# Second out-projection tile prepared among the last input-projection units, and the two blocks of the second half swapped

## The chip, the cores and the metric

The kernel runs on one core of a Trainium2 chip. The metric is the time of one execution in device microseconds (us); lower is better. TensorE (PE) does the matrix products, VectorE (DVE) and ScalarE (ACT) the elementwise work, GpSimd (POOL) small powers and masks, SyncE (SP) issues the DMA transfers.

## The reference

One layer of a hybrid backbone runs over 256 context tokens and 2048 latent tokens of width 1024. Each token is normalised and modulated, and one input projection makes z, the SSD input xbc, dt, and the three conformer inputs ga, gb and gsil. The SSD group scans in both directions; the conformer group convolves. Both meet in one output projection:

```
h = rms_norm(x, g_pre) * (1 + scale) + shift
z, xbc, dt_raw, ga, gb, gsil = split(h @ w_in)
y_ssd  = rms_norm((scan_fwd + scan_bwd + d_skip * xs) * silu(z), norm_g)
y_conf = silu(layer_norm(depthwise_conv(ga * sigmoid(gb)))) * silu(gsil)
out = x + gate * rms_norm(concat(y_ssd, y_conf) @ w_out, g_post)
```

The backward scan runs from the last token to the first. The final scan states of the context are outputs as well.

## The kernel before

All matrix products are made of three float32r products each (high x high, low x high, high x low), so every weight exists as a high part (wh, woh) and a low part (wl, wol).

**Tokens.** 18 tiles of 128 tokens lie in five blocks (`TOK`, `BNS`): block 0 is the context, blocks 1 to 4 are 512 latent tokens each. The input projection runs in two halves, blocks 1, 2, 0 and then 3, 4 (`ORDER`). The normalised input of a block (hh and hl) lies in one of three buffer pools, `hps[SLOT[b]]`. When a pool is closed (`ph_b[...]`), its space goes to what is opened next, once its last reader is done.

**Input projection.** A unit makes 128 output channels for every block of the half, 24 matmuls of 128x512 a block (`mm_cm`). `silu_unit` is such a unit for z and gsil: Tanh on ScalarE, a product on VectorE (tile sth), and a store to a DRAM buffer (zs or gs). The helper yields after each k, so the matmuls of a block are followed by its Tanh and store only when the unit is taken up again. The last three gs units of the second half (`last`, j = 5, 6, 7) run block by block: all three for the first block, then all three for the second.

**Out-projection.** Tiles go backwards through the latent tokens, 17, 16, ... 2, then 1, 0 (`order`); tiles 17 and 16 both lie in block 4. For each tile the kernel

- loads y, z, the decays el, ct and the stored state st (`ssd_load`, `st_load`),
- adds the carried backward state Sb: `state_mm` (16 matmuls, banks qo), `y_state`, then `y_gate` and `y_sum` (product with z, squares, their sum over channels, tile zr), `state_decay` and `state_add`,
- loads the conformer output cn and normalises it: `conf_load`, `conf_sum`, `conf_mean` (bank cm), `conf_centre`, `conf_square`, `conf_sqsum` (tile nq),
- gets the two scale factors in `norms` (matmuls to pm, a power on POOL) and `spread` (matmuls to pn), applies them in `ssd_scale` and `conf_scale`, then `conf_silu` (Silu on ScalarE) and `conf_gate` with the gate gsl that `gs_load` loads back from gs,
- splits the results in high and low parts (yh, yl and ph, pl), and multiplies with 16 weights, 8 with yh, yl and 8 with ph, pl (`out_part`).

Weights are loaded by `load_wo`: a load to a staging buffer wst, a cast to woh on ScalarE and a subtraction to wol on VectorE. wst shares its two tags, of two buffers each, with yh and yl; even weights use the one, odd weights the other. Weights 0 to 8 come during the input projection; 9 to 15 go into pool wo4, which takes the space of the input projection's pools after the last unit. Buffers nq and gsl exist once, cn, v, y and z twice.

**Order.** Up to the loop over `order` the kernel is scheduled when it is built: a planner with an estimate of each instruction's duration orders the instructions of each engine and queue, the earlier in the program first among those that it holds ready. The order is then fixed, and each engine and queue works through its own. In the loop VectorE, ScalarE and TensorE keep program order (`V.on = S.on = T.on = True`); those instructions carry line 77 in the profile. At the start of a tile the loop does the first weight, then `norms` of the next tile.

Of the kernel before, what the change touches and what calls it, by code (L numbers as in the profile page):

```python
# [27 lines left out]
TOK = (0, 256, 768, 1280, 1792)  # L28
BNS = (256, 512, 512, 512, 512)
ORDER = ((1, 2, 0), (3, 4))  # L30
SLOT = (0, 1, 2, 1, 2)
RAWO = (2, 260, 772, 130, 642)
NF = 3
PREP = 16
Z0, XBC0, DT0, GA0, GB0, GS0 = 0, 1024, 2560, 2592, 3616, 4640
# [26 lines left out]
def take(gen, n):  # L62
    for _ in range(n):
        yield next(gen, None)
# [16 lines left out]
def backbone_kernel(ctx, tc, xa, xt_in, cols, rows, wconv, conf_b, gp_row, bg_row, state0, w_mod, w_dt, w_in, w_out,  # L81
# [19 lines left out]
    GS = [dram(f"gs{h}", [D, HT[h] * P]) for h in range(2)]  # L101
# [458 lines left out]
    def silu_unit(half, c0, dst, j, hb, order=None):  # L560
        w = next_w()
        for b in order or ORDER[half]:
            BN, o = BNS[b], TOK[b] - half * HT[0] * P
            ps = bank("mm", f"sp{half}_{c0}_{j}_{b}")
            yield from mm_cm(ps, w, hb[b])
            th = ev(f"sth{half}_{c0}_{j}_{b}")[:, :BN]
            S.activation(th, ps[:, :BN], AF.Tanh, scale=0.5)  # L567
            V.scalar_tensor_tensor(th, th, 1.0, ps[:, :BN], ADD, MUL)  # L568
            DMA.dma_start(dst[half][j * P:(j + 1) * P, o:o + BN], th)
# [308 lines left out]
    def run(gen):  # L878
        for _ in gen:
            pass  # L880
# [5 lines left out]
    hb = {}  # L886
# [30 lines left out]
    xbc_phase(0, first, hb, [hprep(2, hb), hprep(0, hb)], tails, dt_post(0))  # L917
    extra = chain([gate_rows()] + [ctx_conv(j, big) for j in range(4)])
    interleave(post(0, 6), merge(scan(range(9)), 68, extra, 9 + 4 * 13), 90 * 8)
    last = [silu_unit(0, GS0, GS, j, hb, (1, 2, 0)) for j in (6, 7)]  # L920
    prep = hprep(3, hb)
    s = 0
    for b in range(3):
# [67 lines left out]
    def ssd_load(i):  # L991

        first = i == NCTX - 1
        t = sl[i] = {}
        if not first:
            t["ct"] = p1.tile([P, 2, P], F32, tag="ct", name=f"ct{i}", bufs=1)
            DMA.dma_start(t["ct"], xb_slice(i, 10, 2))
            t["el"] = p1.tile([P, 8, P], F32, tag="el", name=f"elb{i}", bufs=1)
            decay_rows(t["el"], i, 1)
        t["y"] = p1.tile([P, 8, P], F32, tag="y", name=f"y{i}", bufs=2)  # L1000
        DMA.dma_start(t["y"].rearrange("p q l -> p (q l)"), YP[i])
        t["z"] = p1.tile([P, 8, P], F32, tag="z", name=f"z{i}", bufs=2)
        DMA.dma_start(t["z"], chan_slice(ZS, i))

    def st_load(i):
        sl[i]["st"] = p1.tile([P, D], F32, tag="st", name=f"stl{i}", bufs=1)
        DMA.dma_start(sl[i]["st"], ST[i])

    def state_mm(i):
        if i != NCTX - 1:  # L1010
            sl[i]["po"] = [bank("ss", f"qo{i}{g}") for g in range(2)]
            for g, po in enumerate(sl[i]["po"]):
                for q in range(4):
                    T.matmul(po[:, q * P:(q + 1) * P], Sb[g][:, q * P:(q + 1) * P], sl[i]["ct"][:, g, :],
                             start=True, stop=True)

    def state_decay(i, g):
        if i != NCTX - 1:
            for h in range(8):
                cs = slice(h * HD, (h + 1) * HD)  # L1020
                S.activation(Sb[g][:, cs], Sb[g][:, cs], AF.Copy, scale=eTb[:, i, 8 * g + h:8 * g + h + 1])

    def state_add(i):
        for g in range(2):
            sg = sl[i]["st"][:, g * 512:(g + 1) * 512]
            if i == NCTX - 1:
                V.tensor_copy(Sb[g], sg)
            else:
                V.tensor_tensor(Sb[g], Sb[g], sg, ADD)

    def y_state(i):
        if i != NCTX - 1:
            el, y = sl[i]["el"], sl[i]["y"]
            for g, po in enumerate(sl[i]["po"]):
                gs = slice(4 * g, 4 * g + 4)
                V.tensor_tensor(el[:, gs, :], el[:, gs, :], y8(po), MUL)
            V.tensor_tensor(y, y, el, ADD)

    def y_gate(i):
        y, z = sl[i]["y"], sl[i]["z"]  # L1040
        V.tensor_tensor(y, y, z, MUL)
        S.activation(z, y, AF.Square)

    def y_sum(i):
        z = sl[i]["z"]
        zr = p1.tile([P, P], F32, tag="zr", name=f"zr{i}", bufs=1)
        return sl[i]["y"], sum8(zr, z[:, 0:4, :], z)
# [6 lines left out]
    def norms(i, yz, nq):  # L1054

        pm = bank("ss", f"pm{i}")
        src = [(c, e, t[1]) for c, e, t in ((0, 4.0 * EPS, yz), (1, EPS, nq)) if t]
        for c, e, t in src:
            T.matmul(pm[:, c:c + 1], t, ones[:, 0:1], start=True, stop=True)
        rs = []  # L1060
        for c, e, t in src:
            ms = p1.tile([P, 1], F32, tag=f"ms{c}", name=f"yms{i}{c}", bufs=2)
            V.tensor_scalar(ms, pm[:, c:c + 1], 1.0 / D, e, MUL, ADD)
            rs.append((c, rstd_of(p1, ms, f"yr{i}{c}")))
        return rs

    def spread(i, rs):
        pb = bank("ss", f"pn{i}")
        for c, r in rs:
            T.matmul(pb[:, c * P:(c + 1) * P], r.to_broadcast([P, P]), ident, start=True, stop=True)  # L1070
        return pb
# [7 lines left out]
    def lo(t):  # L1079
        V.tensor_tensor(t[1], t[2], t[0].bitcast(F32), SUB)  # L1080
# [6 lines left out]
    order = list(range(NT - 1, NCTX - 1, -1)) + [1, 0]  # L1087
# [8 lines left out]
    def conf_load(i):  # L1096
        n = p2.tile([P, 8, P], F32, tag="cn", name=f"cn{i}", bufs=2)
        DMA.dma_start(n, CV[:, i * P:(i + 1) * P].rearrange("(c p) t -> p c t", p=P))
        return n

    def conf_sum(i, n):
        v = p2.tile([P, 8, P], F32, tag="v", name=f"v{i}", bufs=2)
        return v, sum8(v[:, 0, :], v[:, 0:4, :], n)

    def conf_mean(i, t):
        mean = bank("ss", f"cm{i}")[:, 0:P]
        T.matmul(mean, ones, t, start=True, stop=True)
        return mean

    def conf_centre(n, mean):  # L1110
        V.scalar_tensor_tensor(n, rows8(mean), -1.0 / D, n, MUL, ADD)

    def conf_square(v, n):
        S.activation(v, n, AF.Square)
        return v

    def conf_sqsum(i, v):
        return v, sum8(p2.tile([P, P], F32, tag="nq", name=f"nq{i}", bufs=1), v[:, 0:4, :], v)

    def gs_load(i):  # L1120
        gs = p2.tile([P, 8, P], F32, tag="gs", name=f"gsl{i}", bufs=1)
        DMA.dma_start(gs, chan_slice(GS, i))
        return gs

    def conf_scale(n, pb):
        V.tensor_tensor(n, n, rows8(pb[:, P:2 * P]), MUL)

    def conf_silu(n, v):
        for k in range(8):
            S.activation(v[:, k, :], n[:, k, :], AF.Silu, bias=cv[:, C_LNB + k:C_LNB + k + 1],  # L1130
                         scale=cv[:, C_LNG + k:C_LNG + k + 1])

    def conf_gate(v, gs):
        V.scalar_tensor_tensor(v, v, 0.5, gs, MUL, MUL)
# [46 lines left out]
    i = order[0]  # L1181
# [7 lines left out]
    yz = y_sum(i)  # L1189
    for g in range(2):  # L1190
        state_decay(i, g)
    state_add(i)
    run(take(blocks, 5))
    for k in range(6, 9):
        load_wo(k, wo2)
        run(take(blocks, 8))
    run(blocks)
    last = [silu_unit(1, GS0, GS, j, hb) for j in range(5, 8)]
    for b in range(2):
        for m, u in enumerate(last):  # L1200
            run(take(u, 8))
            if b == 0 and m == 1:
                rs = norms(i, yz, None)
            if b == 1 and m == 0:
                ssd_scale(i, yz[0], spread(i, rs))
                yh = hl(p0, "y", 2, i, yz[0])
                lo(yh)
                ph_b[1].close()
                p2 = ph_1.enter_context(tc.tile_pool(name="p2", bufs=1))
                n = conf_load(i)  # L1210
                v, t = conf_sum(i, n)
                conf_centre(n, conf_mean(i, t))
    for u in last:
        run(u)
    v, nq = conf_sqsum(i, conf_square(v, n))
    conf_scale(n, spread(i, norms(i, None, (v, nq))))
    gs = gs_load(i)
    conf_silu(n, v)
    conf_gate(v, gs)
    ph_b[2].close()  # L1220
    ph_h.close()
    p3 = ph_1.enter_context(tc.tile_pool(name="p3", bufs=1))
# [1 line left out]
    for k in range(9, 16):  # L1224
        load_wo(k, wo4)
    load_gg(0)
    i = order[1]
    ssd_load(i)
    st_load(i)
    n = conf_load(i)  # L1230
    state_mm(i)
    y_state(i)
    y_gate(i)
    yz = y_sum(i)
    for g in range(2):
        state_decay(i, g)
    v2, t = conf_sum(i, n)
    conf_centre(n, conf_mean(i, t))
    nq = conf_sqsum(i, conf_square(v2, n))
    gs = gs_load(i)  # L1240
    ssd_load(order[2])
    n2 = conf_load(order[2])
    V.on = S.on = T.on = True
    for a, i in enumerate(order):
        last = a + 1 == NT
# [5 lines left out]
        rs = None if last else norms(nxt, yz, nq)  # L1251
# [7 lines left out]
        if nx2 is not None:  # L1259
            st_load(nx2)  # L1260
            v2, t = conf_sum(nx2, n2)
# [5 lines left out]
        if nxt is not None:  # L1267
# [4 lines left out]
            v = nq[0]  # L1272
# [18 lines left out]
        if nx2 is not None:  # L1291
            y_gate(nx2)
            state_decay(nx2, 1)
            gs = gs_load(nx2)
            nq = conf_sqsum(nx2, v2)
        if a:
            finish_add(order[a - 1])
        if nx2 is not None:
            yz = y_sum(nx2)
        if a + 3 < NT:  # L1300
            ssd_load(order[a + 3])
            n, n2 = n2, conf_load(order[a + 3])
        else:
            n = n2
# [72 lines left out]
```

## Time and profile before

| | |
|---|---|
| median of 3 runs | 1872.1 us (1870.85 to 1872.3) |
| profiled execution | 1872.28 us, span from first to last instruction 1870.5 us |
| TensorE granted clock, mean | 0.984 |
| PE busy | 1808.1 us, 97% of the span |
| DVE, ACT, POOL busy | 1203.1, 863.8, 175.9 us |
| DMA | 375.22 MB, mean 201 GB/s |
| input projection's last unit matmul | at 1404.67 us |
| first out-projection matmul | at 1408.31 us |

Rows of a timeline are: start, duration, engine, line, operation, tile written <- tiles read, and in brackets the idle time of the engine just before, with what ended it. SPq and ACTq are the queues of SyncE and ScalarE. A row with a count (x2) merges neighbours of the same kind. Rows of a chain are: start, duration, what the end of the program was waiting for then. Rows of a stretch are: stretch, its length, then the busy time of each engine with its number of instructions, the granted TensorE clock, the DMA engines' busy share and GB/s.

### The profile page before, as it was taken

Reading aid. Unit: us, or ns where it says so; the run is one execution under the profiler, and the core shown is the slowest. Engines: PE = TensorE matmul, PEld = TensorE weight load, DVE = VectorE, ACT = ScalarE, POOL = GpSimd, SP = SyncE. Lnnn points to the kernel's source line nnn. Section 1 sums busy time; section 2 is a strip of 40 time slices with the busy share of each in tenths; the row PEclk is TensorE's granted clock in tenths of the full one; section 3 lists DMA queues with packets and bytes.
Section 4 is the critical chain, followed back from the end, with each engine's and each line's share of the span. In section 5 each row is a group of like instructions: output and inputs, shape, how many; then the busy total and the mean of one; then the engine's idle time right before and its main releaser. Section 6 shows DMA issues by size and latency. Waiting matters only on the chain.

```text
span 1870.5 us, 30012 instructions
## 1 busy us (share of the span) xinstructions
PE 1808.1 (97%) x11223; PEld 1493.1 (80%) x11223; DVE 1203.1 (64%) x1841; ACT 863.8 (46%) x1956; POOL 175.9 (9%) x281
## 2 busy tenths in 40 slices
PE   7899999999999999999998989999997999999998
PEld 4788887788888888888876767777886888888887
DVE  2477887785555553577587845666347777777773
ACT  3646424455445441644224545553326454444441
POOL 0002001111101100100001111110000111111110
PEclk9899999999999999999999999999998999999999
DMA  8656575576566654545589798895967656666632
GB/s 298 219 199 210 203 241 181 175 254 219 195 217 211 226 196 169 167 155 189 170 200 233 199 251 229 258 244 175 331 189 209 183 167 174 172 171 178 182 106 79
DMA packets 305309, 375.22 MB, mean 201 GB/s; under 512 B 85254, under 2 KB 204678, under 8 KB 305164
## 3 DMA queue, kind: packets, MB, share of 16 engines
q1 hardware_dynamic: 284428, 335.56, 58.1%
q10 hardware_dynamic: 20736, 37.76, 7.1%
q8 instruction: 88, 1.44, 0.3%
q14 instruction: 57, 0.47, 0.1%
HBM read 243.66 MB, written 129.59 MB: 200 GB/s over the span
## 4 chain that ended last, share of the span: by engine, by line
PE 85%; DMA 7%; DVE 4%; ACT 1%; issue 1%; SPq 1%; POOL 0%; POOLq 0%; DVEq 0%; ACTq 0%
PE op L77 21%; PE sp L391 7%; PE sp L392 7%; PE sp L393 7%; PE xp L391 5%; PE xp L392 5%; PE xp L393 5%; PE ga L391 3%; PE ga L393 2%; PE ga L392 2%; PE gb L391 2%; PE gb L393 2%; PE gb L392 2%; DMA lb<-lt 2%; PE py L732 2%; DVE cg L608 2%
## 5 line engine op out<-in xcount | busy, mean ns | idle before, releaser
L696 ACT ACTIVATE lb<-lb,WB 128x128 f32<-128x128 f32 x576 | 184.3, 391 | 167.7 <-POOL lb L688 162.1
L391 PE MATMUL sp<-hh,wh 128*128 128x512 f32 (+1 forms) x640 | 238.5, 373 | 0.0
L392 PE MATMUL sp<-hl,wh 128*128 128x512 f32 (+1 forms) x640 | 236.0, 369 | 0.0
L393 PE MATMUL sp<-hh,wl 128*128 128x512 f32 (+1 forms) x640 | 235.8, 368 | 0.0
L391 PE MATMUL xp<-hh,wh 128*128 128x512 f32 (+1 forms) x480 | 179.3, 375 | 6.1 <-ACT wh L366 4.9
L688 POOL TENSOR_SCALAR_AFFINE_SELECT lb<-lb 128x512 f32<-128x512 f32 x144 | 112.6, 786 | 714.2 <-ACT el L685 366.7
L393 PE MATMUL xp<-hh,wl 128*128 128x512 f32 (+1 forms) x480 | 179.0, 373 | 0.0
L392 PE MATMUL xp<-hl,wh 128*128 128x512 f32 (+1 forms) x480 | 178.9, 373 | 0.0
L488 DVE SCALAR_TENSOR_TENSOR cva<-raw,cwh,cva 128x1280 f32<-128x1280 f32 (+1 forms) x96 | 142.1, 1488 | 19.7 <-ACT cva L482 17.9
L391 PEld LDWEIGHTS sp<-hh,wh 128*128 128x128 f32 x640 | 120.6, 189 | 20.8 <-DVE sth L568 0.4
L393 PEld LDWEIGHTS sp<-hh,wl 128*128 128x128 f32 x640 | 120.6, 188 | 20.7
L392 PEld LDWEIGHTS sp<-hl,wh 128*128 128x128 f32 x640 | 120.7, 189 | 19.8
L391 PE MATMUL ga<-hh,wh 128*128 128x512 f32 (+1 forms) x320 | 122.0, 381 | 6.8 <-DMA wh<-whd 6.3
L391 PE MATMUL gb<-hh,wh 128*128 128x512 f32 (+1 forms) x320 | 121.4, 379 | 5.3 <-DVE gth L555 5.3
L393 PE MATMUL ga<-hh,wl 128*128 128x512 f32 (+1 forms) x320 | 119.4, 373 | 0.5 <-DMA wl<-wld 0.5
L392 PE MATMUL gb<-hl,wh 128*128 128x512 f32 (+1 forms) x320 | 119.6, 374 | 0.0
L393 PE MATMUL gb<-hh,wl 128*128 128x512 f32 (+1 forms) x320 | 119.6, 374 | 0.0
L392 PE MATMUL ga<-hl,wh 128*128 128x512 f32 (+1 forms) x320 | 119.2, 373 | 0.0
L568 DVE SCALAR_TENSOR_TENSOR sth<-sth,sp 128x512 f32<-128x512 f32 (+1 forms) x80 | 50.4, 630 | 97.3 <-ACT sth L567 96.9
L391 PEld LDWEIGHTS xp<-hh,wh 128*128 128x128 f32 x480 | 92.1, 192 | 23.2 <-ACT wh L366 5.5
L608 DVE SCALAR_TENSOR_TENSOR cg<-cg,cv 128x256 f32<-128x256 f32 x240 | 107.6, 487 | 0.6
L392 PEld LDWEIGHTS xp<-hl,wh 128*128 128x128 f32 x480 | 91.7, 191 | 15.7 <-DVE hl L312 0.4
(252 smaller groups left out, 3745.8 us busy)
## 6 DMA issues: line engine op xcount, KB each, us to landing
lb<-lt ACTq DMA_DIRECT2D x144, 256.0 KB, 4.5
wr<-in_w_in SPq DMA_DIRECT2D x88, 256.0 KB, 4.7
whd<-wh SPq DMA_DIRECT2D x44, 512.0 KB, 3.6
wld<-wl SPq DMA_DIRECT2D x44, 512.0 KB, 5.2
wh<-whd SPq DMA_DIRECT2D x44, 512.0 KB, 4.6
wl<-wld SPq DMA_DIRECT2D x44, 512.0 KB, 5.8
xT<-xb SPq DMA_DIRECT2D x18, 512.0 KB, 5.0
yp<-yg SPq DMA_DIRECT2D x36, 256.0 KB, 4.3
```

Of the source, the lines that this page charges most:

```text
L77: return lambda *a, **k: self._tc.keep_in_program_order(f(*a, **k))
L391: T.matmul(ps[:, :BN], wh[:, k, :], hh[:, k, :], start=(k == 0), stop=False)
L392: T.matmul(ps[:, :BN], wh[:, k, :], hl[:, k, :], start=False, stop=False)
L393: T.matmul(ps[:, :BN], wl[:, k, :], hh[:, k, :], start=False, stop=(k == KT - 1))
L488: V.scalar_tensor_tensor(a[:, :n], raw[:, t:t + n], cwh[:, ct * 5 + t:ct * 5 + t + 1], a[:, :n], MUL, ADD)
L568: V.scalar_tensor_tensor(th, th, 1.0, ps[:, :BN], ADD, MUL)
L608: V.scalar_tensor_tensor(acc, g[:, t:t + 256], cv[:, w0 + t:w0 + t + 1], acc, MUL, ADD)
L688: G.affine_select(E[g, hq, d], E[g, hq, d], pattern=[[0, 4], [sg, P]], compare_op=ALU.is_ge, fill=NEG, base=0, channel_multiplier=-sg)
L696: S.activation(lb[:, h, :], lb[:, h, :], AF.Exp, bias=WB[:, i, c + h:c + h + 1])
L732: T.matmul(py[g][j * HD:(j + 1) * HD, q * P:(q + 1) * P], xt[g][:, h * HD:(h + 1) * HD], E[g, hq, 0][:, t, :], start=True, stop=True)
```

## The change

Tile 17 is `order[0]` (i), tile 16 is `order[1]` (i1).

- `SLOT` gives block 3 the pool that block 4 had, and the other way round. The last units of the second half do block 4 before block 3, and those of the first half block 2 before block 1, so that the pool that comes free first is the one that is taken first, as before.
- `ssd_load` and `st_load` of tile 16 stand right after tile 17's `state_add`, no longer behind the weight loads.
- `state_mm`, `y_state` and `y_gate` of tile 16 stand after the second unit of the first block, its `y_sum` and `state_decay` after the third, where tile 17's `ssd_scale` and the split into yh, yl now stand too (they stood one unit later).
- Pool p2 is opened after the third unit of the first block. Both tiles' `conf_load`, `conf_sum`, `conf_mean`, `conf_centre` and `conf_square` stand there, and tile 17's `conf_sqsum`.
- Among the second block's units come tile 17's `norms` with tile 16's `conf_sqsum`, then tile 17's `spread`, `conf_scale` and `conf_silu`, then tile 17's `gs_load` and `conf_gate` and tile 16's `gs_load`. Tile 17's part of this stood behind the last unit, tile 16's behind the weight loads.

Nothing is added to or left out of the computation, and the loop is the same.

```diff
-SLOT = (0, 1, 2, 1, 2)
+SLOT = (0, 1, 2, 2, 1)
...
-    last = [silu_unit(0, GS0, GS, j, hb, (1, 2, 0)) for j in (6, 7)]
+    last = [silu_unit(0, GS0, GS, j, hb, (2, 1, 0)) for j in (6, 7)]
...
     state_add(i)
+    i1 = order[1]
+    ssd_load(i1)
+    st_load(i1)
     run(take(blocks, 5))
...
-    last = [silu_unit(1, GS0, GS, j, hb) for j in range(5, 8)]
+    last = [silu_unit(1, GS0, GS, j, hb, (4, 3)) for j in range(5, 8)]
     for b in range(2):
         for m, u in enumerate(last):
             run(take(u, 8))
             if b == 0 and m == 1:
                 rs = norms(i, yz, None)
-            if b == 1 and m == 0:
+                state_mm(i1)
+                y_state(i1)
+                y_gate(i1)
+            if b == 0 and m == 2:
                 ssd_scale(i, yz[0], spread(i, rs))
                 yh = hl(p0, "y", 2, i, yz[0])
                 lo(yh)
+                yz = y_sum(i1)
+                for g in range(2):
+                    state_decay(i1, g)
                 ph_b[1].close()
                 p2 = ph_1.enter_context(tc.tile_pool(name="p2", bufs=1))
-                n = conf_load(i)
-                v, t = conf_sum(i, n)
-                conf_centre(n, conf_mean(i, t))
+                nn = [conf_load(i), conf_load(i1)]
+                vv = [conf_sum(j, n) for j, n in zip((i, i1), nn)]
+                for (v, t), j, n in zip(vv, (i, i1), nn):
+                    conf_centre(n, conf_mean(j, t))
+                    conf_square(v, n)
+                nq = conf_sqsum(i, vv[0][0])
+            if b == 1 and m == 0:
+                rs = norms(i, None, nq)
+                nq = conf_sqsum(i1, vv[1][0])
+            if b == 1 and m == 1:
+                n, v = nn[0], vv[0][0]
+                conf_scale(n, spread(i, rs))
+                conf_silu(n, v)
+            if b == 1 and m == 2:
+                gs = gs_load(i)
+                conf_gate(v, gs)
+                n = nn[1]
+                gs = gs_load(i1)
     for u in last:
         run(u)
-    v, nq = conf_sqsum(i, conf_square(v, n))
-    conf_scale(n, spread(i, norms(i, None, (v, nq))))
-    gs = gs_load(i)
-    conf_silu(n, v)
-    conf_gate(v, gs)
     ph_b[2].close()
     ph_h.close()
...
     load_gg(0)
-    i = order[1]
-    ssd_load(i)
-    st_load(i)
-    n = conf_load(i)
-    state_mm(i)
-    y_state(i)
-    y_gate(i)
-    yz = y_sum(i)
-    for g in range(2):
-        state_decay(i, g)
-    v2, t = conf_sum(i, n)
-    conf_centre(n, conf_mean(i, t))
-    nq = conf_sqsum(i, conf_square(v2, n))
-    gs = gs_load(i)
     ssd_load(order[2])
```

## The prediction, made before the changed kernel ran

> **What bounds the kernel now.** I read the page first, then the chain of work that ended last, then stretches around the place that the diff touches, then each engine's timeline there. TensorE (PE) is busy nearly throughout, so only time in which PE stands still, or runs slowly, can be won. The page's first row, and the chain where it leaves PE:
>
> ```profile
> PE 1808.1 (97%) x11223; PEld 1493.1 (80%) x11223; DVE 1203.1 (64%) x1841; ACT 863.8 (46%) x1956; POOL 175.9 (9%) x281
> ...
> 1406.44 5.36 DMA gs<-sth
> 1411.85 4.33 DMA gsl<-gs
> 1417.42 2.36 DVE wol L976 x2
> 1422.20 0.98 PE pm L77 x4
> ```
>
> Between the last input-projection unit and the first out-projection tile the chain runs over two transfers in a row: the store of the last gate block, then the load of it back. The stretches (us, PE, PEld, DVE, ACT, POOL, granted clock, DMA share):
>
> ```profile
> 1389.00:1409.94 20.94, 20.06 (x101) 16.63 (x99) 13.59 (x21) 6.91 (x16) 0.55 (x1) 1.00 0.69 208
> 1409.94:1422.20 12.26, 0.00 (x1) 0.03 (x1) 8.38 (x12) 10.00 (x20) 0.00 (x0) 0.60 0.97 234
> 1422.20:1426.40 4.20, 4.20 (x13) 3.52 (x14) 1.60 (x4) 2.10 (x2) 0.22 (x1) 0.54 0.94 312
> ...
> 1447.50:1472.40 24.90, 24.90 (x124) 20.95 (x123) 19.10 (x30) 13.19 (x36) 2.67 (x3) 1.00 0.75 196
> ```
>
> PE does nothing for 12.26 us, and the 4.2 us behind it run at a clock of 0.54. The last row is one whole out-projection tile later: no gap. PE's own timeline gives the marks:
>
> ```profile
> 1404.67 0.39 PE L393 MATMUL sp<-hh,wl 128*128 128x512 f32 x1
> 1404.90 0.28 PE L1059 MATMUL pm<-ones,nq 128*128 128x1 f32 x2
> 1406.06 0.49 PE L1070 MATMUL pn<-ident,yr 128*128 128x128 f32 x2 [0.88 <-POOL yr L148]
> 1406.38 1.95 PE L1014 MATMUL qo<-ct,Sb 128*128 128x128 f32 x16
> 1408.17 0.39 PE L1107 MATMUL cm<-v,ones 128*128 128x128 f32 x2
> 1408.31 0.70 PE L77 MATMUL op<-woh,yh 128*128 128x512 f32 x2
> ...
> 1422.20 0.56 PE L77 MATMUL pm<-ones,zr 128*128 128x1 f32 x2 [12.26 <-DVE zr L986]
> ...
> 1447.56 0.61 PE L77 MATMUL op<-woh,yh 128*128 128x512 f32 x2
> ...
> 1461.39 0.70 PE L77 MATMUL op<-woh,ph 128*128 128x512 f32 x2
> ...
> 1471.49 0.62 PE L77 MATMUL op<-wol,ph 128*128 128x512 f32 x2
> 1472.40 0.61 PE L77 MATMUL op<-woh,yh 128*128 128x512 f32 x2
> ```
>
> The first tile (17) takes 1447.56 - 1408.31 = 39.25 us, the next 1472.40 - 1447.56 = 24.84. The excess, 14.41, is the wait of 12.26 and 2.15 of slow clock. PE waits for zr, nq of tile 16, the second tile, because the loop keeps program order and wants them 1.4 us after its start. What delayed them:
>
> ```profile
> 1409.33 1.28 ACT L1130 ACT_TABLE_LOAD   x1
> 1410.62 3.18 ACT L1130 ACTIVATE v<-cn,cv 128x128 f32<-128x128 f32 x8
> ...
> 1416.28 1.23 DVE L1134 SCALAR_TENSOR_TENSOR v<-v,gsl 128x1024 f32<-128x1024 f32 x1 [3.70 <-DMA gsl<-gs]
> ...
> 1421.57 0.28 DVE L986 TENSOR_TENSOR nq<-v 128x128 f32<-128x128 f32 x1
> ```
>
> **The change, part by part.**
>
> *Loads of tile 16.* Their move up costs and wins nothing: SyncE's queue issues them early already, ct, st and both cn here, the cn pair the moment the first block's buffer is free (L1098 is the load, x2 both tiles):
>
> ```profile
> 1358.64 0.39 SPq L997 DMA_DIRECT2D ct<-xb  x1
> ...
> 1362.52 0.57 SPq L1007 DMA_DIRECT2D stl<-st  x1
> ...
> 1388.24 1.00 SPq L1098 DMA_DIRECT2D cn<-cv  x2
> ...
> 1396.70 0.38 PE L1107 MATMUL cm<-v,ones 128*128 128x128 f32 x2
> ```
>
> The fourth row is tile 17's mean, slipped between unit matmuls with no wait beside it: the pattern that the change extends.
>
> *The swapped blocks.* Both tiles lie in block 4, now stored first; its last unit ends three units (3 x 24 matmuls at 0.23 us, some 16 us) before the last matmul, at about 1388 us. So 5.36 + 4.33 us of store and load leave the chain of tile 17's gate. SLOT swaps two equal 512-token buffers; the order in the first half only mirrors this. Zero for both: the same matmuls hide the same loads. Unhidden, either could cost one transfer, about 5 us.
>
> *Tile 16's PE work* (qo 16 matmuls, cm) and tile 17's pm and pn go ahead of the last unit matmuls. PE still does them: from 1404.90 to 1408.31 is 3.41 us, 0.88 of it waiting, so 2.53 us move ahead and the last unit matmul moves from 1404.67 to 1407.20. The loop starts at 1408.31 - 0.88 = 1407.43.
>
> *VectorE, ScalarE and POOL* do the same instructions earlier. Of VectorE's, tile 16's state part (four operations of up to 1.23 us, and a sum) goes where it is nearly idle, and its conformer part into the stretch above where 7.35 us are free:
>
> ```profile
> 1380.00:1390.00 10.00, 10.00 (x47) 8.30 (x46) 1.53 (x3) 1.20 (x2) 0.55 (x1) 1.00 0.12 38
> ...
> 1417.53 0.37 SPq L1122 DMA_DIRECT2D gsl<-gs  x1
> ```
>
> Two waits are added. nq has one buffer, so tile 16's sum of squares waits for tile 17's pm, with VectorE's later work behind it. The gate load gsl has one buffer too, so tile 16's waits on SyncE's queue for tile 17's gate, and the last store or the staging loads may stand behind it; today that load (second row) went out at 1417.53, as the gate ended (1416.28 + 1.23). I take zero for both: up to 5.85 us of lateness inside tile 17 is covered by the weights, next; past it, each us costs one.
>
> Ceiling so far: 14.41 + 0.88 = 15.29 us.
>
> *What is late next: weights 9 to 15 of the out-projection.* Their tiles take the space of the input-projection pools, and ScalarE's sequencer waits for it; then each staging buffer waits for the subtraction two weights earlier:
>
> ```profile
> L975 ACTq EVENT_SEMAPHORE  x3: 17/38/249, 1411.5 to 1411.9; - x3
> ...
> 1415.14 1.97 ACT L975 CAST woh<-wst 128x1024 fp32r<-128x1024 f32 x2
> ...
> 1418.67 1.48 SPq L969 DMA_DIRECT2D wst<-in_w_out  x2
> ...
> 1426.06 0.33 SPq L969 DMA_DIRECT2D wst<-in_w_out  x1
> ...
> 1429.66 2.69 SPq L969 DMA_DIRECT2D wst<-in_w_out  x2
> ...
> 1424.80 1.23 DVE L976 TENSOR_TENSOR wol<-wst,woh 128x1024 fp32r<-128x1024 f32 x1 [2.75 <-ACT woh L975]
> ...
> 1428.42 1.21 DVE L976 TENSOR_TENSOR wol<-wst,woh 128x1024 fp32r<-128x1024 f32 x1
> ...
> 1430.77 1.23 DVE L976 TENSOR_TENSOR wol<-wst,woh 128x1024 fp32r<-128x1024 f32 x1 [0.54 <-ACT woh L975]
> ...
> 1435.38 1.23 DVE L976 TENSOR_TENSOR wol<-wst,woh 128x1024 fp32r<-128x1024 f32 x1 [0.46 <-ACT woh L975]
> 1436.79 1.23 DVE L976 TENSOR_TENSOR wol<-wst,woh 128x1024 fp32r<-128x1024 f32 x1 [0.18 <-ACT woh L975]
> ```
>
> The load at 1426.06, for one, follows the subtraction that ends at 1424.80 + 1.23 = 1426.03. The semaphores came at 1411.5 to 1411.9; the last gate store landed at 1406.44 + 5.36 = 1411.80, so I take it that the casts wait for that store (its source buffer lies in the space). It landed 7.13 us after the last unit matmul, and this link moves with the matmul: 1407.20 + 7.13 = 1414.33 after the change, about when the casts run today. From the first cast to the end of the last subtraction is 1438.02 - 1415.14 = 22.88 us, a relay of four transfers on two buffers; it would end at 1437.21. PE reaches wol of weight 15 at 1471.49 - 1447.56 = 23.93 us after a tile's start, that is at 1431.36. Wait: 5.85 us. Bounds: 0, where the buffers that tile 17's yh and yl hold serve as staging once PE has used them (1461.39 - 1447.56 = 13.83 into the tile, at 1421.26), and 5.85 + 5.74 = 11.6, where the last store is held on ScalarE as well (rival 2). I take 5.85, nearest to the rows: today no staging load uses those buffers either.
>
> Cut by weight (12 is ready 14.49 us after the first cast, 13 after 16.86, 14 after 21.47; PE uses one every 1.38 us, 10.1 us for 7 1/3), the wait falls into about 1.6, 1.0 and 3.2 us. The Trainium skill, "TensorE: Matmul & The Clock Gate", What's actually happening, has the clock halved after an idle window of about 3.4 us and full after as long a busy one. The trace agrees on the first gap, 0.60 and then 0.54 granted. By that rule these pieces would keep the clock; joined, they would cost another 2.15, and the sum would be 1865.
>
> **Sum.** 15.29 - 5.85 = 9.44 us off the profiled execution's own 1872.28, so 1862.84. That execution is 0.18 above the median of the runs, 1872.1; forecast 1862.7.
>
> **The rivals.**
>
> 1. *The weights come in time* (the freed yh/yl buffers serve, or casts start sooner): the whole 15.29, 1857.0. For it: two free buffers are just what the relay lacks. Against: they come free at 1421.26, after four of the seven weights are under way, and the next tile's yh and yl want them too.
>
> 2. *The casts start later still.* Silu of tile 17 now stands ahead of the last units' Tanh in the program. Silu needed a table load (1.28) after a long run of Tanh; interleaved, the last Tanh may wait for 3.18 of Silu and two loads, 5.74 us in all, and the last store, the casts and PE's wait go with it one for one: down to 1868.6. Against: the planner may put Tanh first. The Trainium skill, "ScalarE: Activation LUTs", What ACT_TABLE_LOAD costs, gives a switch about 2.66 us including a drain; by that 8.5 us, and 1871.3. The trace differs: 1409.33 + 1.28 is 1410.61, and Silu starts at 1410.62.
>
> 3. *No change.* The relay ends over 5.8 us later than I have it, say with casts queued behind tile 17's Silu, ph and tile 16's work on ScalarE: first cast near 1420, 1868.6 to 1875. Each us of cast delay is a us of time.
>
> 4. *Slower: PE's queue is held inside the last units.* PE issues in a fixed order. If the planner puts tile 17's mean, pm and pn where it believes them ready, and the data come later, everything behind stops, and last matmul, store and weights all move along. From the cn issue at 1388.24 to pn at 1406.06 is 17.82 us; held for all of it, 1862.84 + 17.82 = 1880.7. It decides from 9.44 us of such waits (13.2 for a loss of 0.2%). For it: pn waited 0.88 even today. Against: cm and tile 17's first pn waited nothing, and 16 us of unit matmuls are there to fill.
>
> **How the numbers follow.** A measurement of this kernel tells about 0.2%, 3.7 us, from no change. Chances: forecast, 1860 to 1865.5, 0.40; rival 1, 1856.5 to 1860, 0.25; rival 2, 1865.5 to 1868.4, 0.17; rival 3, 0.10; rival 4, 0.08. Faster 0.40 + 0.25 + 0.17 = 0.82, same 0.10, slower 0.08. The range that leaves out rivals 3 and 4 is 1856.5 to 1868.5.
>
> **What the profile after would show.** Right: the chain no longer has gsl in it; no PE wait for zr; qo and cm of tile 16 among the unit matmuls; the clock at 1.00 through the change-over; the first tile taking 24.84 us plus a wait for woh or wol of weights 12 to 15; the later tiles still 24.84. Wrong: a wait of PE among the last six unit blocks (rival 4), more than one ACT_TABLE_LOAD near Silu with the last Tanh behind it (rival 2), or no wait for wol at all (rival 1). What would break the forecast whole is a different plan of the queues elsewhere, seen as changed times before 1350.

## The result, and the profile after

The changed kernel is slower: 1883.74 us (1882.67 to 1886.02) against 1872.2 (1870.85 to 1874.19), a ratio of 1.0062 [1.0045, 1.008]. The forecast was 1862.7, faster. The profiled execution took 1884.29, its span is 12.0 us longer than that of before (1882.5 against 1870.5), and all 12 us have come by the end of the first out-projection tile (1459.57 against 1447.56). Busy times on the page are those of before within 4 us; TensorE does the same matmuls:

```profile
PE 1810.8 (96%) x11223; PEld 1495.9 (79%) x11223; DVE 1202.5 (64%) x1841; ACT 864.1 (46%) x1956; POOL 171.9 (9%) x281
```

TensorE's timeline at the change-over:

```profile
1399.94 0.38 PE L1107 MATMUL cm<-v,ones 128*128 128x128 f32 x2
...
1406.09 0.39 PE L393 MATMUL sp<-hh,wl 128*128 128x512 f32 x1
1406.32 0.39 PE L77 MATMUL op<-woh,yh 128*128 128x512 f32 x1
1406.54 0.28 PE L1059 MATMUL pm<-ones,nq 128*128 128x1 f32 x2
1407.70 0.49 PE L1070 MATMUL pn<-ident,yr 128*128 128x128 f32 x2 [0.88 <-POOL yr L148]
1407.94 0.48 PE L77 MATMUL op<-woh,yh 128*128 128x512 f32 x1
...
1409.18 0.28 PE L77 MATMUL pm<-ones,zr 128*128 128x1 f32 x2
...
1413.30 0.61 PE L77 MATMUL op<-woh,yl 128*128 128x512 f32 x2
1438.44 1.40 PE L77 MATMUL pn<-ident,yr 128*128 128x128 f32 x4 [24.52 <-POOL yr L148]
...
1459.57 0.62 PE L77 MATMUL op<-woh,yh 128*128 128x512 f32 x2
```

The old wait is gone: pm of zr, which waited 12.26 us, runs at 1409.18 without one. Four weights into the tile comes a new wait, twice as long: pn of tile 16, the second half of the same two factors. It waits for POOL's power yr, which needs yms, the scaled mean square that VectorE makes from pm. The stretches (us, then PE, PEld, DVE, ACT, POOL, granted clock, DMA share, GB/s) show a TensorE that stands still, a clock that drops for it, and a later tile of the same length as before (24.80 us, without a gap):

```profile
1408.00:1413.90 5.90, 5.90 (x29) 4.61 (x27) 1.22 (x1) 4.36 (x9) 0.00 (x0) 1.00 0.69 210
1413.90:1438.40 24.50, 0.02 (x1) 0.00 (x0) 11.40 (x12) 8.27 (x9) 1.54 (x2) 0.60 0.49 150
1438.40:1443.00 4.60, 4.56 (x15) 3.88 (x16) 4.49 (x8) 1.18 (x2) 0.59 (x1) 0.52 0.31 114
1459.60:1484.40 24.80, 24.80 (x123) 20.90 (x122) 18.66 (x28) 12.36 (x33) 2.68 (x3) 1.00 0.56 159
```

VectorE is busy for less than half of the wait (11.40 of 24.50), and yet yms, 0.2 us of work, does not come through. Its timeline says why:

```profile
1414.04 1.22 DVE L1134 SCALAR_TENSOR_TENSOR v<-v,gsl 128x1024 f32<-128x1024 f32 x1 [4.60 <-ACT v L1130]
1415.84 2.36 DVE L976 TENSOR_TENSOR wol<-wst,woh 128x1024 fp32r<-128x1024 f32 x2 [0.57 <-ACT woh L975]
1423.69 2.50 DVE L976 TENSOR_TENSOR wol<-wst,woh 128x1024 fp32r<-128x1024 f32 x2 [5.49 <-ACT woh L975]
1429.52 1.23 DVE L976 TENSOR_TENSOR wol<-wst,woh 128x1024 fp32r<-128x1024 f32 x1 [3.34 <-ACT woh L975]
1431.87 1.23 DVE L976 TENSOR_TENSOR wol<-wst,woh 128x1024 fp32r<-128x1024 f32 x1 [1.12 <-ACT woh L975]
1435.49 1.22 DVE L976 TENSOR_TENSOR wol<-wst,woh 128x1024 fp32r<-128x1024 f32 x1 [2.39 <-ACT woh L975]
1436.63 0.21 DVE L77 TENSOR_SCALAR yms<-pm 128x1 f32<-128x1 f32 x2
```

Its input pm was there before 1410, and it ran at 1436.63: all seven subtractions of weights 9 to 15 stand ahead of it. Each waits (the brackets) for its cast; the first two casts stand behind tile 17's Silu, the other five wait for transfers. Tile 17's gate (1414.04) stands ahead of yms too, but it ends at 1415.26; from there to 1436.63, 21.4 us, nothing but the subtractions stands ahead of yms. Before, only three subtractions stood ahead. This is the row of before's VectorE timeline; of its subtractions shown in the prediction, the one at 1424.80 is the third, and those at 1428.42, 1430.77, 1435.38 and 1436.79 come behind yms, between the loop's own instructions:

```profile
1425.95 0.21 DVE L77 TENSOR_SCALAR yms<-pm 128x1 f32<-128x1 f32 x2
```

The chain of what ended last, after, is the relay (load, cast and subtraction of one weight after the other) and then yms. It runs through the odd weights 9, 11, 13 and 15: from 11 on, the load of each starts as the subtraction of the one before frees its staging buffer:

```profile
1407.86 3.84 DMA gs<-sth
1411.70 2.32 ACT v L1130 x6
...
1414.76 1.05 ACT woh L975
1415.84 1.24 DVE wol L976
1417.09 5.50 DMA wst<-in_w_out
...
1434.41 1.05 ACT woh L975
1435.49 0.98 DVE wol L976
...
1436.63 0.23 DVE yms L77 x2
1436.86 1.53 POOL yr L148
...
1438.44 1.40 PE pn L77 x4
```

The account against before: 12.26 + 2.15 us go, 24.52 and some 2.2 of slow clock (4.60 x 0.48) come: +12.3, where the spans differ by 12.0.

### The profile page after: what moved, and what is told of

Same layout as the page of the kernel before. It is cut to its first block, busy times and chain, and to the rows that moved or that the text cites. A ratio compares the mean times of both kernels' runs of the same rounds, so it can differ in the third digit from the quotient of the medians.

```text
span 1882.5 us, 30016 instructions
## 1 busy us (share of the span) xinstructions
PE 1810.8 (96%) x11223; PEld 1495.9 (79%) x11223; DVE 1202.5 (64%) x1841; ACT 864.1 (46%) x1956; POOL 171.9 (9%) x281
## 4 chain that ended last, share of the span: by engine, by line
PE 79%; DMA 10%; DVE 4%; ACT 3%; issue 3%; POOL 1%; SPq 0%; ACTq 0%; POOLq 0%; DVEq 0%
PE op L77 21%; PE sp L391 7%; PE sp L392 7%; PE sp L393 7%; PE xp L391 4%; PE xp L393 4%; PE xp L392 4%; DMA lb<-lt 3%; PE ga L391 2%; PE ga L393 2%; PE ga L392 2%; PE gb L391 2%; PE gb L393 2%; PE gb L392 2%; DMA xin<-in_xa 2%
## 5 line engine op out<-in xcount | busy, mean ns | idle before, releaser
L688 POOL TENSOR_SCALAR_AFFINE_SELECT lb<-lb 128x512 f32<-128x512 f32 x144 | 108.5, 758 | 718.0 <-ACT el L685 380.3
L700 DVE TENSOR_TENSOR lb<-lb,lb 128x512 f32<-128x512 f32 x72 | 50.2, 698 | 84.6 <-ACT lb L696 68.7
```

The costliest lines, as they stand in the source:

```text
L688: G.affine_select(E[g, hq, d], E[g, hq, d], pattern=[[0, 4], [sg, P]], compare_op=ALU.is_ge, fill=NEG, base=0, channel_multiplier=-sg)
L700: V.tensor_tensor(a, a, E[g, hq, 1], ADD)
```

## Experiments

Theory: the loss is the order on VectorE. The subtractions are waiting work, and what stands behind them waits too, although PE needs no late weight until far into the tile. Rivals: the relay's length alone sets the time wherever its work stands; or the swap of the blocks costs. Runs of one kernel spread over some 7 to 12 us on these chips, and marks shift with them, so ratios and waits are compared, not clock marks. Each ratio is against the kernel before on the same chip.

**e1_hoist** puts tile 16's factors ahead of the weights:

```diff
+    rs0 = norms(i1, yz, nq)
+    state_add(i1)
+    pb0 = spread(i1, rs0)
     for k in range(9, 16):
         load_wo(k, wo4)
```

(the loop uses them for its first tile.)

> Tile 16's norms, state_add and spread stand ahead of the loads of weights 9 to 15 instead of inside the loop. Theory (VectorE's fixed order: all seven wol subtractions stand ahead of the loop's first yms, so the staging relay that ends at 1436.7 us holds everything behind it): pn no longer waits; PE runs on until the next product that sits behind wol of weight 15 on VectorE, the mean cm of tile 15, some 13.7 us into the tile. The wait moves from pn to cm and shrinks from 24.5 to about 17 to 18 us; 6 to 8 us faster than the changed kernel, about 1877. Rival (the weights themselves are what PE lacks): the relay ends where it did, so no gain, 1884. Rival (the loss sits in the last input-projection units): no gain either.

Measured: 1875.49 us, ratio 1.0012 [1.0, 1.0024]. Of the loss of 0.62%, some 0.5% (9 us) comes back, a little more than the 6 to 8 us expected. Of the wait at tile 16's pn 1.67 us are left, now ahead of the loop, and the next instructions of the loop that stand behind the subtractions, pl and tile 15's sums for the mean cm, take its place. TensorE's row, and two of the chain's:

```profile
1441.65 0.80 PE L77 MATMUL cm<-v,ones 128*128 128x128 f32 x2 [11.81 <-DVE v L77]
```

```profile
1437.73 0.98 DVE wol L976
1438.88 1.23 DVE pl L77
```

So PE stops at the first thing that it needs from behind the relay, whichever that is. The wait at cm is shorter than the 17 to 18 us expected. The relay itself took about as long, 20.5 us from the first cast to the end of the last subtraction against 21.95, so its length does not explain 11 us less waiting.

**e2_no_relay** takes the relay away:

```diff
-    wo4 = ph_1.enter_context(tc.tile_pool(name="wo4", bufs=1, side="right"))
     for k in range(9, 16):
-        load_wo(k, wo4)
+        WH[k], WL[k] = WH[k - 8], WL[k - 8]
```

(This kernel leaves out part of `w_out`; the loads, casts and subtractions go with it.)

> The changed kernel without the loads, casts and subtractions of weights 9 to 15; weights 1 to 7 are used in their place, so that part of w_out is left out. Theory: everything lost comes from that relay; PE goes from the last unit into the loop with no wait over 2 us, the first tile takes about 25 to 27 us, and the time is the ceiling of the prediction, 1857 (1855 to 1860). Rival (waits in the last units, or the moved work on VectorE and ScalarE): several us stay, 1865 or more.

Measured: 1861.58, ratio 0.9938 [0.992, 0.9955], 11.6 us below before by the ratio. Without the relay the wait of 24.52 is gone and the change does win, though less than expected (1857) and not the full ceiling of 15.29. TensorE's timeline keeps the 0.88 at pn and shows a new wait:

```profile
1417.78 3.02 PE L77 MATMUL qo<-ct,Sb 128*128 128x128 f32 x16 [2.50 <-DVE Sb L77]
```

The state sum Sb stands in program order behind pl, which waits for tile 17's Silu and gate; and the 16 small matmuls take 3.02 us where e5 has 2.05.

**e3_staging** gives the relay more buffers: weights 11, 12 and 15 are staged in two buffers of the output pool that stand empty until a tile ends.

```diff
-        wr = p0.tile([P, D], F32, tag=("yh", "yl")[k % 2], ...
+        if k in (11, 12, 15):
+            wr = p3.tile([P, D], F32, tag="o", name=f"wst{k}", bufs=2)
+        else:
+            wr = p0.tile([P, D], F32, tag=("yh", "yl")[k % 2], ...
```

> The changed kernel with the staging of weights 11, 12 and 15 in the two result buffers o, which the loop needs only from its second tile; 9, 10, 13, 14 stay on yh and yl. Weights 11 and 12 need not wait for the subtractions of 9 and 10, so the relay has two links of transfers fewer. Theory: last subtraction ends near 1427 to 1429 instead of 1436.7, PE's wait at pn shrinks from 24.5 to about 15 to 17 us, time about 1875 (8 to 10 us less). Rival (the casts' start, not the relay, sets it): under 3 us.

Measured: 1875.98, ratio 1.0016 [1.0003, 1.0028]. The order is that of the change, the relay is shorter (11.8 us instead of 21.95), and pn's wait shrinks with it, about as expected, from 24.52 to 14.93:

```profile
1430.38 1.40 PE L77 MATMUL pn<-ident,yr 128*128 128x128 f32 x4 [14.93 <-POOL yr L148]
```

e1 and e3 together: the wait is the part of the relay that lies between the last thing PE had and the first instruction behind the relay. Moving the instruction or shortening the relay both shorten it. So the pure rival (the relay's length wherever it stands) falls with e1, and that it is only the order falls with e3.

**e4_swap_alone** is the kernel before with `SLOT` and the two unit orders of the change, nothing else.

> The kernel before with the swapped blocks alone (SLOT and both orders), nothing moved. Theory: the gate load of tile 17 no longer waits for the last store, but ScalarE was busy without a break in that gap and the squares of tile 16 stay behind Silu and two casts there, so PE's wait of 12.3 us shrinks by 0 to 4 us: 1868 to 1872. Rival (store and load back in a row set the gap): 8 to 10 us less, 1863.

Measured: 1872.57, ratio 0.9996 [0.9986, 1.0006]. The swap costs and wins nothing. The old wait shrinks a little:

```profile
1423.70 0.56 PE L77 MATMUL pm<-ones,zr 128*128 128x1 f32 x2 [11.04 <-DVE zr L986]
```

The store and load back of tile 17's gate, on the chain of before, were thus not what set the gap by themselves: here the gate waits for Silu (1.25 us) and no longer for its load, and the gap is 11.04 instead of 12.26.

**e5_in_loop** moves the loads of the weights into the first tile of the loop, where VectorE and ScalarE keep program order:

```diff
-    for k in range(9, 16):
-        load_wo(k, wo4)
...
             pb = spread(nxt, rs)
+        if a == 0:
+            load_wo(9, wo4)
+            load_wo(10, wo4)
```

(11 and 12 behind `conf_silu`, 13 to 15 behind `conf_square`.)

> The changed kernel with the loads of weights 9 to 15 written inside the first tile of the loop, where program order holds: 9 and 10 behind state_add and spread, 11 and 12 behind conf_silu, 13 to 15 behind conf_square. Nothing else differs, staging included. Theory (the loss is the order on VectorE, not the weights' lateness as such): pn's wait goes, PE first waits where it uses a late wol, near weight 13 to 15; the first tile ends near 1440 us of the span instead of 1459.6, time 1864 to 1868. Rival (weights late, wherever they stand in the queue): the relay ends where it did or later, 1880 or more.

Measured: 1875.53, ratio 1.0014 [0.9998, 1.003]: missed. The wait at pn is gone, but TensorE's waits now lie elsewhere, and with some small ones at weights (0.17, 0.53, 0.28) they add up to 11.4 us. The clock behind the longest is 0.50 for 5.6 us, some 2.8 us more:

```profile
1421.69 2.05 PE L77 MATMUL qo<-ct,Sb 128*128 128x128 f32 x16 [2.52 <-DVE Sb L77]
...
1441.51 1.22 PE L77 MATMUL op<-woh,ph 128*128 128x512 f32 x2 [5.29 <-ACT woh L77]
...
1453.79 0.35 PE L77 MATMUL pm<-ones,zr 128*128 128x1 f32 x2 [2.58 <-DVE zr L77]
```

Here the weights come too late themselves: a load, its cast and its subtraction are written in one place, and the cast of the late ones stands behind tile 16's own work on ScalarE.

**e6_in_loop_staging** is e5 with e3's staging.

> As the one before, with weights 11, 12 and 15 staged in the o buffers. Theory: the relay no longer ends last, the wait for wol shrinks to 0 to 3 us; VectorE, with seven subtractions of 1.23 us on top of its 19.1 us a tile, is late with zr and nq of tile 15 at the start of the second tile, which costs a few us: 1860 to 1865. Rival (the relay sets the first tile's end even so): no better than the one before.

Measured: 1872.46, ratio 0.999 [0.9978, 1.0003]; missed too. The wait for zr goes, those for Sb and woh stay at 2.52 and 5.31: buffers do not help a cast that its engine reaches late. ScalarE stands ahead of the last three casts, in an earlier instruction of the loop that waits 4.28 us for VectorE:

```profile
1441.19 1.06 ACT L77 ACTIVATE v<-cn 128x1024 f32<-128x1024 f32 x1 [4.28 <-DVE cn L77]
1442.15 2.92 ACT L77 CAST woh<-wst 128x1024 fp32r<-128x1024 f32 x3
```

**e7_ordered**: e6 with `state_add` ahead of pl, and each `load_wo` placed where its engines are free (9 ahead of `lo(pt)`, 10 behind it, 11 ahead of the fifth weight, 12 to 14 ahead of the cast to yhn, 15 behind its low part).

> As the one before, with the first tile's order on VectorE set by need: state_add ahead of pl, wol 9 ahead of pl, 10 to 14 as PE uses them, 15 behind yl. Theory: no wait over 1 us before weight 15; what is left is VectorE's 27.7 us of work in a tile of 24.8, so PE waits 3 to 6 us for zr and nq at the second tile: 1860 to 1864. Rival (VectorE is not the limit): 1857.

Measured: 1870.58, ratio 0.9982 [0.9969, 0.9995]: the time missed its 1860 to 1864. The waits for woh and wol are down to 0.90 and 0.53, and the lateness turns up at the next tile, whose zr now comes late, as VectorE has waited for casts:

```profile
1442.94 0.56 PE L77 MATMUL pm<-ones,zr 128*128 128x1 f32 x2 [6.16 <-DVE zr L77]
```

The clock drops behind it: 0.50 granted in the 6.1 us that follow, some 3 us lost.

**e8_pool_sub**: e7 with the subtractions of weights 12, 14 and 15 on GpSimd.

```diff
-            V.tensor_tensor(wl, wr, wh.bitcast(F32), SUB)
+            (G if k in (12, 14, 15) else V).tensor_tensor(wl, wr, ...
```

> As the one before, with the subtractions of weights 12, 14 and 15 on GpSimd, which is idle there. Theory (VectorE's load is what is left): 3.7 us leave VectorE, the wait at the second tile shrinks by 2 to 4 us: 1858 to 1861. Rival (GpSimd is slower at it, or the two disturb each other, so that PE waits for wol 14 or 15): no gain or a loss of 1 to 3 us.

Measured: 1868.86, ratio 0.9965 [0.995, 0.998], short of the 1858 to 1861 expected. The intervals of e7 and e8 overlap, so a gain from the move is not shown. The wait for zr is 2.50 now, but cm waits 2.77 and wol 1.30. What GpSimd takes over VectorE does not get back: it hands over three subtractions of 1.22 us, and three of the instructions left to it together take 6.2 us longer; see the last section.

**e9_split** keeps e3's staging and splits `load_wo`: the load and the cast stay together, the subtraction (`sub_wo`) gets a place of its own, behind the work that PE needs sooner.

```diff
             S.copy(wh, wr)
-            V.tensor_tensor(wl, wr, wh.bitcast(F32), SUB)
+            late[k] = wl, wr, wh
...
+            load_wo(9, wo4)
+            load_wo(10, wo4)
         pt = hl(p2, "p", 1, i, v)
...
+            state_add(nxt)
+            sub_wo(9)
+            sub_wo(10)
         lo(pt)
```

(casts of 11, 12 behind ph's, 13, 14 ahead of yhn's, 15 behind Silu; `sub_wo` of 11, 12 behind yhn, of 13, 14 behind `conf_silu`, of 15 behind `y_state`.)

> As e7_ordered (all subtractions on VectorE), with cast and subtraction of a weight placed apart: casts 9 to 12 stand on ScalarE right behind tile 17's Silu and ph, so that VectorE need not stand idle for them, and the subtractions follow PE's need. Theory (what is left is VectorE's work plus its idle time in tile 17, then the slow clock after a long PE wait): 2 to 4 us of VectorE's 8 us idle time go, the wait for zr of tile 15 falls from 6.2 to 2 to 4 us, and 2 to 5 us are won against e7_ordered, 0.3 to 0.45% below the kernel before. Rival (the loads of 13 to 15 set it): no gain.

Measured: 1864.68, ratio 0.9957 [0.9941, 0.9973], as expected. Left are waits of 1.05 for wol and of 3.71 for the next zr:

```profile
1446.80 0.35 PE L77 MATMUL pm<-ones,zr 128*128 128x1 f32 x2 [3.71 <-DVE zr L77]
```

**e10_late_norms**: e9, and in the second tile `norms` stands behind the fourth weight and `spread` behind the sixth, so that PE asks for zr later.

```diff
-        rs = None if last else norms(nxt, yz, nq)
+        rs = None if last or a == 1 else norms(nxt, yz, nq)
...
         out_part(pso[i], yh, 1, 4)
+        if a == 1:
+            rs = norms(nxt, yz, nq)
```

> As e9_split, and in the second tile alone PE does its norms behind the fourth weight and its spread behind the sixth, 4 us later, so that VectorE may be late with zr and nq by that. Theory: PE's waits in the first two tiles fall to under 2 us in all and the clock stays at 1.00; the loss of the relay is then hidden whole and the time is that of the kernel without the relay, 0.5 to 0.65% below the kernel before. Rival (VectorE does not catch up, the wait only moves to the products behind, cm or the third tile's norms): no gain against e9_split.

Measured: 1859.74, ratio 0.9925 [0.991, 0.9941]: about 14 us below before, a little more than expected, and by the two ratios 1.4% below the change as made. The clock keeps 1.00 through the whole change-over (two of its stretches; the other four from 1395 to 1455 have 1.00 as well), and besides the 0.88 two waits of 1 us are left:

```profile
1405.00:1415.00 10.00, 9.12 (x48) 7.69 (x47) 4.84 (x9) 5.27 (x11) 2.14 (x3) 1.00 0.85 278
...
1425.00:1435.00 10.00, 8.99 (x40) 7.13 (x39) 9.96 (x11) 7.51 (x19) 0.00 (x0) 1.00 0.63 185
```

```profile
1432.47 0.73 PE L77 MATMUL op<-wol,ph 128*128 128x512 f32 x2 [1.01 <-DVE wol L77]
...
1442.00 2.02 PE L77 MATMUL qo<-ct,Sb 128*128 128x128 f32 x16 [1.04 <-DVE Sb L77]
```

## Why the prediction was wrong

**The step that failed** is the last of the change part by part, "PE reaches wol of weight 15 at ... 1431.36. Wait: 5.85 us", with the sentence before it that "up to 5.85 us of lateness inside tile 17 is covered by the weights". Both take it that a late weight holds PE only where PE uses it. But the relay runs on VectorE and ScalarE, in a fixed order, and whatever stands behind a subtraction in that order is as late as it is. The rows to see this were there: before, yms ran at 1425.95, between the third subtraction and the fourth. I moved the inputs of yms ahead by 13 us (pm at 1409.18 instead of 1422.20) and never asked which subtractions would then stand ahead of it. The Trainium skill, "TensorE: Matmul & The Clock Gate", in the section on the array's architectural detail, calls VectorE's and ScalarE's queues strict first in, first out. The trace agrees, with 0.2 us of ready work held for over 26 us. Whether the 5.85 us at weight 15 would have come by themselves stays open: after the change and in e1 and e3 PE had stopped for something else before it got there.

The error in numbers: the forecast for the profiled execution was 1862.84, measured 1884.29, 21.45 more. The wait is 24.52 instead of 5.85 (18.67), the slow clock behind it 2.2, and the 0.88 at pn, which I had counted as won, is still there: 21.75 in all.

**What held.**
- The ceiling (15.29): e10 reaches 14.1 (interval 11 to 17), with waits of 0.88, 1.01 and 1.04 left. The 0.88 in it was wrongly counted: the prediction has tile 17's pm and pn run ahead of the last unit matmuls, but they came behind them (1406.54 and 1407.70), and between the two PE waits for VectorE and POOL as before.
- Loads and swap at zero: e4 for the swap, and no wait of PE for a load of tile 16 in the trace.
- The loop's start: 1407.43 predicted, and all but one matmul of it from 1407.94 on, behind the 0.88 wait. The last unit matmul came at 1406.09 instead of 1407.20, as pm and pn did not move ahead of it.
- The relay: first cast 1414.76 (1414.33 predicted), last subtraction ended 1436.71 (1437.21). Its size was right; what it holds up was not. That the first cast fits to 0.4 us is in part luck: I had it start as the last gs store lands, but the store landed at 1411.70, 2.6 us earlier than the 1414.33 predicted, and the cast ran when Silu had ended (0.75 us behind it). What the cast's last semaphore stood for is not shown.
- The clock: I took the wait in pieces that would keep it. It came in one piece, and cost the 2.2 us that the prediction gave for that case (2.15).

**The rivals.** Rival 1 (weights in time) did not come, though staging in other buffers, which it rests on, did shorten the relay in e3. Rival 2: there is one table load, and the last Tanh stands ahead of it, so Silu did not delay the last store:

```profile
1406.52 0.60 ACT L567 ACTIVATE sth<-sp 128x512 f32<-128x512 f32 x1 [2.96 <-PE sp L393]
1409.52 1.28 ACT L1130 ACT_TABLE_LOAD   x1 [2.41 <-DVE cn L1126]
...
1414.76 1.99 ACT L975 CAST woh<-wst 128x1024 fp32r<-128x1024 f32 x2 [0.75 <-ACT v L1130]
```

Rival 3 needed a first cast near 1420; it came at 1414.76. Rival 4 has the sign right and the general idea, an engine with a fixed order held by something that is not ready, but the wrong engine and place: the two tiles' cm among the last units wait for nothing (tile 16's is the row at 1399.94, first timeline). Of the marks that I had called right, these came true: no gsl on the chain, no wait for zr, tile 16's qo and cm among the unit matmuls, the later tile at 24.80. The clock of 1.00 and the wait at wol did not.

**Open:** why the planner, which orders VectorE up to the loop, put all seven subtractions ahead of the loop's yms after the change and three before. Its estimates of the transfers may be the place, but no run varied them. Nor was the 0.88 at pn tried.

## What to carry to other kernels

A late instruction is to be priced not only where its result is used, but also where the first instruction queued behind it on its own engine is needed: write down for each engine what stands behind each thing that waits for a transfer. When a stall is removed, the work that used to run inside it changes its place in those queues. Split helpers that chain a load, a cast and a subtraction, place each part by when the next engine needs it, and expect several steps until the gain shows: here the ratio went from 1.0062 to 1.0012 by order alone, to 1.0016 by staging alone, and to 0.9925 with order, staging, split and late norms together. The steps between, from e5 to e9, are small, and the intervals of neighbours overlap.

## What the hardware showed that I had not expected

In e8, VectorE stood while GpSimd subtracted. GpSimd's and VectorE's timelines:

```profile
1419.37 2.81 POOL L979 TENSOR_TENSOR wol<-wst,woh 128x1024 fp32r<-128x1024 f32 x1 [8.69 <-DMA gsl<-gs]
1425.66 2.39 POOL L979 TENSOR_TENSOR wol<-wst,woh 128x1024 fp32r<-128x1024 f32 x1 [3.48 <-ACT woh L77]
```

```profile
1419.87 2.85 DVE L77 TENSOR_TENSOR v<-cn 128x512 f32<-128x512 f32 x1
...
1425.69 3.43 DVE L77 TENSOR_TENSOR wol<-wst,woh 128x1024 fp32r<-128x1024 f32 x1
```

The first VectorE instruction took 0.68 in e7 and 2.85 here, and ends 0.54 us after GpSimd's; the subtraction takes 1.22 elsewhere and 3.43 here, ending 1.07 after GpSimd's 1428.05. So each seems to have done nearly all of its work once GpSimd had finished. The Trainium skill, "SBUF — State Buffer", Who interferes with whom, says that a VectorE instruction with two inputs in SBUF contends with a GpSimd instruction that reads SBUF, and calls the ports they share an exclusive lock. The trace agrees, at some 2.2 us for each of these two.

The clock's loss behind a short wait is not the same each time. Behind 2.50 us in e2 the granted clock was 0.68 over 5.3 us and the 16 qo matmuls took 3.02; behind 2.52 in e5 it was 1.00 and they took 2.05; behind 1.67 in e1 it was 0.61 over 4.4 us. The waits of 6.16 (e7), 12.26 (before) and 24.52 (after) cost 2 to 3 us each.
